# A bidirectional state-space scan in an encoder trunk: the order of the state product, one PSUM bank, the norm's second half and two empty steps

## The chip, the cores and the metric

The kernel runs on one core of a Trainium2 chip, as one program. The metric is the device time of one execution in microseconds (us); lower is better. The engines are named as in the profile: PE (TensorE, matmuls; PEld is its weight load), DVE (VectorE), ACT (ScalarE), POOL (GpSimd) and SP, whose queue issues most transfers. Each runs its own list of instructions in order and waits on semaphores. Matmuls write to PSUM, which has eight banks here, each holding one tile of 128 x 512 float32.

## The reference

Two layers (DEPTH) of an encoder trunk work on 16 meta tokens and 1024 tokens of 1024 features (L = 1040). Each layer normalises, projects once, splits the columns over four groups (pooling, a 2-D Fourier transform, a bidirectional state-space scan, attention), gates them, projects back and adds to the residual. The change touches the scan. Cut to what matters:

```python
def ssd_direction(xh, dt, a, bm, cm):          # one direction, in chunks
    xdt = xh * dt; cs = cumsum(dt * a)         # within a chunk
    cb = einsum("bclgn,bcsgn->bcgls", cc, bc)  # C.B, masked, times exp(cs_t - cs_s)
    y_diag = einsum("bcgrls,bcsgrp->bclgrp", cb * lmat, xdt)
    chunk_states = einsum("bclgn,bcgrl,bclgrp->bcgrpn", bc, exp(cs_end - cs), xdt)
    h_next = h * exp(cs_end) + chunk_states    # carried from chunk to chunk
    y_off = einsum("bclgn,bcgrpn,bcgrl->bclgrp", cc, h_before_chunk, exp(cs))
    return y_diag + y_off

def ssd_mixer(...):
    y = forward + flipped backward + d_skip * x
    y = y * silu(z)
    return rmsnorm(y, norm_w)                  # over 512 features
```

Both directions have eight heads of 64 in two groups with 128 states; the step sizes `dt` are a softplus of a projection.

## The kernel before

Features lie on the partitions, tokens along the rows, and float32 products are made of three matmuls on rounded halves (`mm3`, L133 to L135). Tokens go in three chunks of 348, 346 and 346 for the projections and in NQ = 10 chunks of QC = 104 for the scan.

**Who sets the order.** The functions are generators that yield after each step. `weave` takes steps of several streams in turn by weights; `stage(gen, steps, n)` weaves a stream with n pieces of `fill2`, the output projection of the other groups (each piece 12 matmuls L133 to L135, then an add L337 or, for the attention group, a copy L334 and an add L335, between transfers). On top of that the framework orders each engine's instructions itself when the program is built, by its own estimate of times and of when buffers come free. So a line that stands later in the code can come earlier on an engine, and the order has to be read from the built program.

**PSUM.** `ps(tag)` hands out banks. The tag `mm` has two banks of its own; `sc`, `pv` and `xx` have one each. Three spare banks, y0, y1 and y2, are lent to tags by SPARE, one entry per stage. The last entry is that of the scan: y0 and y2 go to `xx`, y1 to `sc`. Tiles are named after the bank, so a tile of `xx` shows as psxx or psy in the profile, where numbers are left out.

**The step sizes** (`ssd_dt`, part D of the stream `fill` that runs beside attention): five passes of two chunks each. A pass loads its projection (L715), goes through a chain of some 20 small DVE and ACT instructions up to L744, transposes on PE (L748, L749), copies (L751) and stores.

**The backward scan** (`ssd_bwd`, nine steps): `ssd_tok` transposes a chunk of x into `sc` (L771) and of B into `xx` (L774), and copies the latter to one of three small buffers (L776). `ssd_state` scales x (L786), makes the state product on PE (L789) and adds it to the decayed state (POOL L795, DVE L796). Its buffers come from a pool that the projections of the other groups hold in part.

**The forward scan** (`ssd_fwd`) goes through two kinds of steps in turn. `prepare(q)`: transposes, the C-B product in `xx` (L854), its two masked copies (L858, L859), eight minima and exponentials (DVE L861, ACT L862), eight pairs of scaled copies and multiply-adds (ACT L865, DVE L866), and one product on POOL (L867). `finish(q)`: the backward and forward state's part of the output (`ssd_off`, PE L803, in `sc` and `pv`), evacuated by DVE L878 and L881; the state product, also in `pv`; POOL's add L886; the product with x on PE in `xx` (L892), added by L893; the skip term L895.

**The norm** (`ssd_fin`) runs once per token chunk, in two halves. The first gates and sums squares (L928 to L932). The second sums over partitions on PE (L935), takes the root by Ln and Exp on ACT (`rstd`, L139 to L146) and scales (L939). `silu_` (L300) needs a table of ACT other than Ln and Exp do, and asks for theirs again behind it (L301).

In both layers the last part of the scan is woven with the output projection of its own first two token chunks (`tail`).

Of the kernel before, what the change touches and what calls it, by code (L numbers as in the profile page):

```python
# [28 lines left out]
NQ = L // QC  # L29
# [23 lines left out]
def hybrid_trunk(ctx: ExitStack, tc: tile.TileContext, io, out, depth=DEPTH):  # L53
# [20 lines left out]
    NBIG, NBB = 30, 5  # L74
    WB = (4, 5)
    PB, KB, NPF, NACC = 2, 3, 14, 4
    SPARE = (('xx', 'xx', 'mm'), ('sc', 'sc', 'mm'), ('xx', 'mm', 'xx'), ('xx', 'sc', 'xx'))
    GK = 2
    FB = (6, 6, 0, 1, 4, 1, 6, 9)
    GA = (22, 23, 22, 13)  # L80
# [619 lines left out]
    def ssd_dt(l, s):  # L700

        s.csd = drp.tile([NQ, 2, 8, QC], F32, name=nm("csd"))
        s.ecd = drp.tile([NQ, 2, 8, QC], F32, name=nm("ecd"))
        s.ded = drp.tile([2, 8, NQ], F32, name=nm("ded"))
        s.tkd = drp.tile([NQ, QC, 144], F32, name=nm("tkd"))
        R = slice(0, 40)
        a = wp.tile([40, 1], F32, name=nm("a"), tag="a", bufs=1)
        nc.scalar.activation(a, vec(l, V_AL)[R], AF.Exp)
        nc.vector.tensor_scalar(a, a, -1.0, None, op0=ALU.mult)
        for q0 in range(0, NQ, 2):  # L710
            n = 2
            w = n * QC
            v = big()
            x, e, u, dt, t1 = [v[:, i * w:i * w + w] for i in range(5)]
            nc.sync.dma_start(x[R], s.gd["dt"][0, :, q0 * QC:q0 * QC + w])  # L715
            nc.vector.tensor_scalar(x[R], x[R], vec(l, V_DTB)[R], None, op0=ALU.add)
            nc.scalar.activation(e[R], x[R], AF.Abs)
            nc.scalar.activation(e[R], e[R], AF.Exp, scale=-1.0)
            nc.vector.tensor_scalar(u[R], e[R], 1.0, None, op0=ALU.add)
            nc.vector.scalar_tensor_tensor(e[R], u[R], 1.0, e[R], op0=ALU.subtract, op1=ALU.subtract)  # L720
            nc.scalar.activation(u[R], u[R], AF.Ln)
            nc.vector.tensor_tensor(u[R], u[R], e[R], op=ALU.subtract)
            nc.vector.scalar_tensor_tensor(dt[R], x[R], 0.0, u[R], op0=ALU.max, op1=ALU.add)
            nc.vector.tensor_scalar(x[R], dt[R], a, None, op0=ALU.mult)
            nc.vector.memset(t1[32:64], 0.0)
            for i in range(n):
                c = slice(i * QC, (i + 1) * QC)
                nc.vector.tensor_tensor_scan(t1[0:32, c], ones[0:32, :QC], x[0:32, c], 0.0, op0=ALU.mult, op1=ALU.add)
                nc.vector.tensor_tensor_scan(t1[32:40, c][:, ::-1], ones[32:40, :QC], x[32:40, c][:, ::-1], 0.0, op0=ALU.mult, op1=ALU.add)
            by_q = lambda ap: ap.rearrange("p (q t) -> p q t", t=QC)  # L730
            cs = by_q(t1[R])
            ce = wp.tile([40, 4], F32, name=nm("ce"), tag="ce", bufs=2)[:, :n]
            nc.vector.tensor_copy(ce[0:32], cs[0:32, :, QC - 1])
            nc.vector.tensor_copy(ce[32:40], cs[32:40, :, 0])
            nc.vector.tensor_tensor(by_q(e[R]), ce.unsqueeze(2).broadcast_to([40, n, QC]), cs, op=ALU.subtract)
            nc.scalar.activation(e[R], e[R], AF.Exp)
            nc.vector.tensor_tensor(t1[64:104], e[R], dt[R], op=ALU.mult)
            nc.scalar.activation(u[R], t1[R], AF.Exp)
            nc.scalar.activation(ce, ce, AF.Exp)
            for i, r in ((0, slice(0, 8)), (1, slice(32, 40))):  # L740
                nc.sync.dma_start(s.csd[q0:q0 + n, i].rearrange("q r t -> r q t"), by_q(t1[r]))
                nc.sync.dma_start(s.ecd[q0:q0 + n, i].rearrange("q r t -> r q t"), by_q(u[r]))
                nc.sync.dma_start(s.ded[i, :, q0:q0 + n], ce[r])
            nc.vector.tensor_scalar(t1[R], t1[R], -1.0, None, op0=ALU.mult)  # L744
            p = ps("xx")
            for i in range(n):
                c = slice(i * QC, (i + 1) * QC)
                nc.tensor.transpose(p[:QC, 144 * i:144 * i + 104], t1[:104, c], ident[:104, :104])  # L748
                nc.tensor.transpose(p[:QC, 144 * i + 104:144 * i + 144], dt[:40, c], ident[:40, :40])  # L749
            t = sm("s")  # L750
            nc.scalar.copy(t[:QC, :144 * n], p[:QC, :144 * n])  # L751
            nc.sync.dma_start(s.tkd[q0:q0 + n].rearrange("q t c -> t q c"), t[:QC, :144 * n].rearrange("t (q c) -> t q c", c=144))
            yield
# [81 lines left out]
    def ssd_fwd(l, s):  # L835
# [34 lines left out]
        def finish(q, st):  # L870
            qs = slice(q * QC, (q + 1) * QC)
            xt, xw, bt, rb = ready.pop(q)
            e = vr(big())
            for a in range(2):
                nc.sync.dma_start(e[64 * a:64 * a + 64].rearrange("p (i j) t -> p i j t", i=2), s.ecd[q, :, 4 * a:4 * a + 4].partition_broadcast(64))
            if q < NQ - 1:
                pb = ssd_off(s, q, s.sb[q], "sc")
                nc.vector.tensor_tensor(e[:, 4:8], pb.rearrange("p (j t) -> p j t", t=QC), e[:, 4:8], op=ALU.mult)  # L878
            if q > 0:
                pf = ssd_off(s, q, st, "pv")  # L880
                nc.vector.tensor_tensor(e[:, 0:4], pf.rearrange("p (j t) -> p j t", t=QC), e[:, 0:4], op=ALU.mult)  # L881
            new = None
            if q < NQ - 1:
                new = ssd_state(s, 0, q, xt, bt, st, xw, s.sf[:, 512 * (q % 2):512 * (q % 2) + 512])
            if 0 < q < NQ - 1:
                nc.gpsimd.tensor_tensor(e[:, 0:4], e[:, 0:4], e[:, 4:8], op=ALU.add)  # L886
            y = e[:, 4:8] if q == 0 else e[:, 0:4]
            pd = ps("xx")
            for h in range(8):
                j, a = h // 2, h % 2  # L890
                r = 4 * a + j
                nc.tensor.matmul(pd[64 * a:64 * a + 64, j * QC:(j + 1) * QC], xt[:, h * 64:h * 64 + 64], rb[:, r], start=True, stop=True)  # L892
            nc.vector.tensor_tensor(y, y, pd[:, :4 * QC].rearrange("p (j t) -> p j t", t=QC), op=ALU.add)  # L893
            for j in range(4):
                nc.vector.scalar_tensor_tensor(s.y[j][:, qs], s.xbc[j][:, qs], vec(l, V_DS + j), y[:, j], op0=ALU.mult, op1=ALU.add)  # L895
            return new

        s.sf = big()
        st = norm = None
        for q in range(NQ + 1):  # L900
            if q < NQ:
                prepare(q)
            if norm is not None:
                next(norm, None)
                norm = None
            if q < NQ:
                yield
            if q:
                st = finish(q - 1, st)
                ci = next((i for i, (c0, cw) in enumerate(CH) if (q - 1) * QC < c0 + cw <= q * QC), None)  # L910
                if ci is not None:
                    norm = ssd_fin(l, s, ci)
# [67 lines left out]
    for l in range(depth):  # L980
        s = S()
# [173 lines left out]
```

## Time and profile before

| | |
|---|---|
| median of 3 runs | 2183.52 us (2173.6 to 2186.84) |
| the profiled execution | 2183.98 us, span 2181.9 us |
| mean granted TensorE clock | 0.964 |
| backward scan, layers 0 and 1 | about 860 to 930 and 1935 to 2008 us of the span |
| forward scan | about 930 to 1085 and 2008 to 2160 us |
| step sizes | about 424 to 462 and 1505 to 1543 us |
| matmuls, PE | 11868 records, 2002.1 us busy |

The profile is of one execution. A row of a list of groups reads: line, engine, operation, output and inputs, shape, count, then busy time, mean ns of one, and the idle time of the engine ahead of it with what ended it. A row of a list of waits reads: who waited for whom, us in total, times, longest. Lines are those of the kernel before. In the changed kernel those behind L744 are higher by 2 (so L748, L776, L789, L796, L861, L866, L867, L892 and L893 are L750, L778, L791, L798, L863, L868, L869, L894 and L895 there), the evacuations L878 and L881 are L883 and L886, and the norm's lines are higher by 1.

### The profile page before, as it was taken

To read this page: it belongs to the slowest core of one execution; us is meant where nothing else is said; L and a number is where in the kernel's file an instruction comes from. 1 tells how busy PE (TensorE), PEld (TensorE's weight loads), DVE (VectorE), ACT (ScalarE), POOL (GpSimd) and SP (SyncE) were. 2 spreads that over 40 slices of the span, in tenths; PEclk is the share of its full clock that TensorE was granted. 3 is DMA by queue.
4 is the path that set the end of the run, shared out by engine and by line. 5 is a ranking of instruction groups with operands and counts; after the bars stand their busy time and mean duration, and the time that the engine had idled before them with its cause. 6 is when DMAs were issued, how large, how long until landed. Compare 5 with 4: busy or idle time off the path is not lost. (4 is left out here: it accounts for less than half of the span.)

```text
span 2181.9 us, 33618 instructions
## 1 busy us (share of the span) xinstructions
PE 2002.1 (92%) x11868; PEld 1755.1 (80%) x11868; DVE 1323.7 (61%) x2614; ACT 1004.6 (46%) x2191; POOL 642.0 (29%) x642
## 2 busy tenths in 40 slices
PE   6699999989999999988976999999999999988888
PEld 5498888867899868877864988888778997878778
DVE  6373535558566355689864735256576554466996
ACT  5335254444443456346443353444435425463562
POOL 3005235135131220245220142441442304112550
PEclk9799999999999999999997999999999999999999
DMA  4321222113224478776743212121223335776666
GB/s 131 103 86 61 59 66 74 36 56 95 94 81 137 126 217 267 195 186 187 223 125 108 88 59 68 64 63 34 76 81 99 124 113 149 246 231 179 176 190 188
DMA packets 170374, 269.48 MB, mean 124 GB/s; under 512 B 21522, under 2 KB 117334, under 8 KB 170206
## 3 DMA queue, kind: packets, MB, share of 16 engines
q1 hardware_dynamic: 167550, 258.01, 39.0%
q0 software_dynamic: 2656, 9.33, 1.7%
q8 instruction: 93, 1.52, 0.3%
q14 instruction: 75, 0.61, 0.1%
HBM read 189.27 MB, written 73.77 MB: 121 GB/s over the span
## 5 line engine op out<-in xcount | busy, mean ns | idle before, releaser
L133 PE MATMUL psmm<-big,wh 128*128 128x346 f32 (+2 forms) x1920 | 639.8, 333 | 27.0 <-ACT sms L334 9.2
L134 PE MATMUL psmm<-big,wh 128*128 128x346 f32 (+2 forms) x1920 | 629.7, 328 | 7.7 <-DVE big L130 4.0
L135 PE MATMUL psmm<-big,wl 128*128 128x346 f32 (+2 forms) x1920 | 626.3, 326 | 2.0 <-DVE wl L130 2.0
L646 POOL TENSOR_TENSOR acc<-acc,pf 116x346 f32<-116x346 f32 (+4 forms) x336 | 343.9, 1048 | 531.6 <-ACT pf L637 531.5
L133 PEld LDWEIGHTS psmm<-big,wh 128*128 128x128 f32 x1920 | 367.9, 192 | 62.2 <-issue 21.7
L134 PEld LDWEIGHTS psmm<-big,wh 128*128 128x128 f32 x1920 | 368.2, 192 | 19.5 <-DVE big L130 8.4
L135 PEld LDWEIGHTS psmm<-big,wl 128*128 128x128 f32 x1920 | 368.3, 192 | 6.3 <-DVE wl L130 2.6
L130 DVE TENSOR_TENSOR wl<-wr,wh 128x512 fp32r<-128x512 f32 x232 | 182.8, 792 | 215.2 <-ACT wh L129 214.2
L129 ACT CAST wh<-wr 128x512 fp32r<-128x512 f32 (+1 forms) x236 | 145.0, 616 | 270.9 <-PE psmm L134 216.7
L133 PE MATMUL psy<-big,wh 128*128 128x346 f32 (+2 forms) x672 | 224.1, 334 | 0.0
L134 PE MATMUL psy<-big,wh 128*128 128x346 f32 (+2 forms) x672 | 223.1, 332 | 1.1 <-POOL big L182 0.7
L135 PE MATMUL psy<-big,wl 128*128 128x346 f32 (+2 forms) x672 | 219.2, 326 | 0.0
L606 DVE TENSOR_REDUCE mx<-psy 128x1 f32<-128x346 f32 (+3 forms) x272 | 132.8, 512 | 56.1 <-PE psy L605 55.4
L637 ACT ACTIVATE pf<-psy 116x346 f32<-116x346 f32 (+4 forms) x288 | 125.6, 457 | 80.3 <-PE psy L635 77.2
L656 PE MATMUL pspv<-pf,vt 116*64 116x346 f32 (+5 forms) x864 | 160.6, 463 | 0.0
L133 PEld LDWEIGHTS psy<-big,wh 128*128 128x128 f32 x672 | 129.9, 193 | 10.9 <-issue 8.8
L134 PEld LDWEIGHTS psy<-big,wh 128*128 128x128 f32 x672 | 130.0, 193 | 8.5 <-DVE big L130 2.8
L135 PEld LDWEIGHTS psy<-big,wl 128*128 128x128 f32 x672 | 130.3, 194 | 1.3 <-issue 0.8
L606 DVE TENSOR_REDUCE mx<-pssc 128x1 f32<-128x346 f32 (+3 forms) x136 | 69.9, 514 | 69.3 <-PE pssc L605 68.4
L337 DVE TENSOR_TENSOR sms<-sms,psmm 128x346 f32<-128x346 f32 (+2 forms) x128 | 65.1, 511 | 73.7 <-PE psmm L135 43.8
L656 PEld LDWEIGHTS pspv<-pf,vt 116*64 116x64 f32 (+1 forms) x864 | 58.6, 136 | 61.5 <-issue 24.0
L634 PE MATMUL psy<-big,big 128*116 128x346 f32 (+4 forms) x288 | 95.8, 334 | 8.1 <-DVE mx L606 7.2
(285 smaller groups left out, 3331.3 us busy)
## 6 DMA issues: line engine op xcount, KB each, us to landing
wr<-w SPq DMA_DIRECT2D x248, 256.0 KB
hd<-sms SPq DMA_DIRECT2D x112, 173.0 KB
sms<-hd SPq DMA_DIRECT2D x112, 173.0 KB
bb<-csd SPq DMA_DIRECT2D x40, 338.0 KB
md<-big SPq DMA_DIRECT2D x24, 520.0 KB
gd<-sms SPq DMA_DIRECT2D x64, 173.0 KB
big<-gd SPq DMA_DIRECT2D x16, 520.0 KB
big<-md SPq DMA_DIRECT2D x16, 520.0 KB
```

What stands on the lines that cost most here:

```text
L129: nc.scalar.copy(hi, src)
L130: nc.vector.tensor_tensor(lo, src, f(hi), op=ALU.subtract)
L133: nc.tensor.matmul(out_ps, ah, bh, start=start, stop=False)
L134: nc.tensor.matmul(out_ps, ah, bl, start=False, stop=False)
L135: nc.tensor.matmul(out_ps, al, bh, start=False, stop=stop)
L337: nc.vector.tensor_tensor(ht, ht, p[:, :cw], op=ALU.add)
L606: nc.vector.tensor_reduce(mx[:qn, q, e, ci:ci + 1], p[:qn, :cw], axis=AX.X, op=ALU.max)
L634: nc.tensor.matmul(p[:n, :cw], k1[:, k0:k0 + n], s1[e][:, cs], start=True, stop=False)
L637: nc.scalar.activation(pf[:n, :cw], p[:n, :cw], AF.Exp, scale=0.125)
L646: nc.gpsimd.tensor_tensor(accs[c0, e][:n, :cw], accs[c0, e][:n, :cw], pf[:n, :cw], op=ALU.add)
L656: nc.tensor.matmul(hold["pv"][64 * e:64 * e + 64, :cw], s.vt[:n, k, v, :], pfs[e][:n, :cw], start=(k == 0), stop=(k == len(KTS) - 1))
```

## The change

Four edits. The last entry of SPARE lends y2 to `pv` instead of `xx`: in the scan `pv` has two banks and `xx` two (one and three before). In `finish` the state product and its update are issued ahead of the backward and forward parts of the output instead of behind them. The norm's second half is issued after the next `finish` instead of ahead of it, and behind the yield. `ssd_dt` yields twice, with nothing issued between, ahead of the transposes.

```diff
-    SPARE = (('xx', 'xx', 'mm'), ('sc', 'sc', 'mm'), ('xx', 'mm', 'xx'), ('xx', 'sc', 'xx'))
+    SPARE = (('xx', 'xx', 'mm'), ('sc', 'sc', 'mm'), ('xx', 'mm', 'xx'), ('xx', 'sc', 'pv'))
@@ ssd_dt
             nc.vector.tensor_scalar(t1[R], t1[R], -1.0, None, op0=ALU.mult)
+            yield
+            yield
             p = ps("xx")
@@ finish
+            new = None
+            if q < NQ - 1:
+                new = ssd_state(s, 0, q, xt, bt, st, xw, s.sf[:, 512 * (q % 2):512 * (q % 2) + 512])
             if q < NQ - 1:
                 pb = ssd_off(s, q, s.sb[q], "sc")
                 nc.vector.tensor_tensor(e[:, 4:8], pb.rearrange("p (j t) -> p j t", t=QC), e[:, 4:8], op=ALU.mult)
             if q > 0:
                 pf = ssd_off(s, q, st, "pv")
                 nc.vector.tensor_tensor(e[:, 0:4], pf.rearrange("p (j t) -> p j t", t=QC), e[:, 0:4], op=ALU.mult)
-            new = None
-            if q < NQ - 1:
-                new = ssd_state(s, 0, q, xt, bt, st, xw, s.sf[:, 512 * (q % 2):512 * (q % 2) + 512])
@@ the loop over q
             if q < NQ:
                 prepare(q)
-            if norm is not None:
-                next(norm, None)
-                norm = None
-            if q < NQ:
                 yield
             if q:
                 st = finish(q - 1, st)
+                if norm is not None:
+                    next(norm, None)
+                    norm = None
```

What the built program makes of it, at three places.

On PE, in layer 0, near the end of the backward scan. L774 (now L776) are transposes of B, L771 (L773) of x, L789 (L791) state products; psmm marks fill. L854 (L856) on psxx_8916 is the C-B product of forward step 0. Before:

```order
L774 MATMUL psy_8909<-ct,big_8176 104x128
L774 MATMUL psy_8909<-ct,big_8177 104x128
L789 MATMUL pspv_8694<-big_8691,smq_8689 128x256 x2
L771 MATMUL pssc_8777<-ct,big_8172 104x128
L771 MATMUL pssc_8777<-ct,big_8173 104x128
L771 MATMUL pssc_8777<-ct,big_8174 104x128
L771 MATMUL pssc_8777<-ct,big_8175 104x128
L854 MATMUL psxx_8916<-big_8178,big_8176 104x104
L854 MATMUL psxx_8916<-big_8179,big_8177 104x104
L133 MATMUL psmm_8666<-big_8224,wh_8606 128x346
L134 MATMUL psmm_8666<-big_8225,wh_8606 128x346
```

Now:

```order
L134 MATMUL psmm_9227<-big_8240,wh_9132 128x346
L135 MATMUL psmm_9227<-big_8239,wl_9133 128x346
L133 MATMUL psmm_9288<-big_8548,wh_9282 128x348
L856 MATMUL psxx_8916<-big_8178,big_8176 104x104
L856 MATMUL psxx_8916<-big_8179,big_8177 104x104
L805 MATMUL pssc_9093<-big_8178,big_8847 128x104
L791 MATMUL psy_9089<-big_8914,smq_8912 128x256 x2
```

Step 0's C-B product has moved from ahead of a long run of fill (the one that writes psmm_8666 to psmm_9227) to behind it, next to the first `finish`. The products of steps 1 and 2, which stood within that run, have moved behind it as well, and layer 1 has the same.

On DVE, in layer 0, what follows those products. L858 and L859 (now L860, L861) are the masked copies, L866 (L868) the multiply-adds, bb_8901 belongs to step 0 and bb_8990 to step 1; L337 evacuates fill, L130 splits its weights. Before, at the start of the run of fill:

```order
L858 TENSOR_TENSOR cfb_8919<-psxx_8916,ct 104x208
L859 TENSOR_TENSOR cfb_8919<-psxx_8916,ct 104x208
L337 TENSOR_TENSOR sms_8664<-sms_8664,psmm_8666 128x346
L130 TENSOR_TENSOR wl_9133<-wr_9130,wh_9132 128x512
L866 SCALAR_TENSOR_TENSOR bb_8901<-cfb_8919,big_8166,bb_8901 104x104 x4
L337 TENSOR_TENSOR sms_8706<-sms_8706,psmm_8708 128x348
L866 SCALAR_TENSOR_TENSOR bb_8901<-cfb_8919,big_8166,bb_8901 104x104 x4
```

Now, behind it (L798 adds a state product, L883 evacuates a backward part, L788 scales x):

```order
L337 TENSOR_TENSOR sms_9225<-sms_9225,psmm_9227 128x346
L860 TENSOR_TENSOR cfb_8919<-psxx_8916,ct 104x208
L861 TENSOR_TENSOR cfb_8919<-psxx_8916,ct 104x208
L788 TENSOR_TENSOR big_9003<-big_9003,big_8166 104x4x64 x2
L130 TENSOR_TENSOR wl_9848<-wr_9845,wh_9847 128x512
L868 SCALAR_TENSOR_TENSOR bb_8901<-cfb_8919,big_8166,bb_8901 104x104 x8
L883 TENSOR_TENSOR big_9084<-pssc_9093,big_9084 128x416
L860 TENSOR_TENSOR cfb_9008<-psxx_9005,ct 104x208
L861 TENSOR_TENSOR cfb_9008<-psxx_9005,ct 104x208
L798 TENSOR_TENSOR big_8899<-big_8899,pspv_9247 128x512
L868 SCALAR_TENSOR_TENSOR bb_8990<-cfb_9008,big_8166,bb_8990 104x104 x5
```

The work of steps 0 and 1 has moved from among the evacuations of fill to among the first `finish` steps.

On ACT, in layer 0, at the second norm. z is gated by L300; L139 and L141 are Ln and Exp of the norm; L334 copies fill. Before:

```order
L300 ACT_TABLE_LOAD
L300 ACTIVATE z_10182<-z_10182 128x4x346
L334 COPY sms_9841<-psmm_9828 128x346
L301 ACT_TABLE_LOAD
L776 COPY smq_9882<-psy_9879 104x256
```

Now:

```order
L300 ACT_TABLE_LOAD
L300 ACTIVATE z_10182<-z_10182 128x4x346
L334 COPY sms_9750<-psmm_9737 128x348
L334 COPY sms_9769<-psmm_9756 128x346
L139 ACT_TABLE_LOAD
L139 ACTIVATE smn_9813<-psxx_9811,epst 128x348
L778 COPY smq_9882<-psy_9879 104x256
L141 ACT_TABLE_LOAD
L141 ACTIVATE smn_9815<-smn_9813 128x348
```

The first norm's Ln and Exp now follow the second norm's gate directly, ahead of the preload L301, and each loads a table of its own. The whole program has 68 table loads, 55 before. At the step-size transposes 59 and 60 matmuls (layers 0 and 1) stood between the last score product of the first attention pair and the first transpose; now 62 and 61 do.

## The prediction

> **What bounds the kernel now.** I read the page's shares first, then the stretches, then who waits for whom. The page says that TensorE is the busiest engine:
>
> ```profile
> PE 2002.1 (92%) x11868; PEld 1755.1 (80%) x11868; DVE 1323.7 (61%) x2614; ACT 1004.6 (46%) x2191; POOL 642.0 (29%) x642
> ```
>
> An average hides stages, so here are the stretches around the scan. The columns are length, then busy time (and instructions) of PE, PEld, DVE, ACT and POOL, the granted clock, the DMA share and GB/s.
>
> ```profile
> 896.00:928.00 32.00, 29.20 (x186) 28.53 (x184) 18.09 (x48) 11.56 (x35) 6.39 (x6) 1.00 0.75 201
> 928.00:1030.00 102.00, 85.63 (x591) 77.44 (x591) 95.11 (x216) 54.47 (x152) 52.47 (x49) 0.95 0.66 185
> 1030.00:1060.00 30.00, 29.01 (x196) 26.98 (x195) 28.28 (x63) 18.46 (x44) 11.46 (x9) 0.95 0.65 179
> 1060.00:1085.00 25.00, 21.12 (x132) 20.08 (x131) 16.27 (x38) 8.99 (x19) 2.19 (x3) 0.93 0.91 273
> 1975.00:2006.00 31.00, 28.36 (x173) 27.64 (x171) 15.47 (x41) 8.47 (x25) 5.58 (x5) 0.94 0.74 202
> 2006.00:2115.00 109.00, 92.63 (x658) 84.00 (x658) 100.04 (x233) 62.31 (x177) 57.17 (x51) 0.95 0.70 183
> 2115.00:2160.00 45.00, 39.61 (x253) 36.82 (x252) 37.23 (x79) 18.00 (x36) 8.35 (x8) 0.92 0.69 194
> ```
>
> In the forward scans (928 to 1030 and 2006 to 2115) VectorE (DVE) is busy 93% and 92%, TensorE (PE) only 84% and 85%: **the scan is bound by DVE**. Just ahead of each scan (896 to 928, 1975 to 2006) it is the other way round: PE runs fill at 91%, and DVE has 14 and 16 us free. The change aims at PE's waits:
>
> ```profile
> PE pspv L789 <- DVE big L881: 18.2, 9, 4.3
> PE psy L935 <- DVE sms L932: 9.2, 4, 2.9
> PE psxx L748 <- DVE big L744: 6.9, 4, 3.7
> ```
>
> The first is the state product waiting for its one bank, the second the norm's sum, the third the step-size transposes: 34.3 us in all, 1.6% of the span. But the first two waits are waits for an engine that is itself full. Removing them lets PE come earlier to the next thing that DVE has not done. What the scan can gain is DVE's own idle time:
>
> ```profile
> DVE big L893 <- POOL big L886: 2.4, 2, 1.2
> DVE sms L337 <- DMA sms<-hd: 2.1, 1, 2.1
> DVE big L878 <- DMA big<-ecd: 2.0, 2, 1.7
> DVE big L786 <- ACT big L851: 1.9, 2, 1.7
> DVE big L796 <- PE pspv L789: 0.6, 2, 0.4
> ...
> DVE big L893 <- POOL big L886: 3.4, 3, 1.2
> DVE big L878 <- DMA big<-ecd: 3.0, 2, 2.0
> DVE big L786 <- ACT big L851: 1.6, 1, 1.6
> ```
>
> These are DVE's waits in the two scans, the first five from layer 0. Only 0.6 us of them is a wait for the state product (L796), which the new order brings forward; the rest is for POOL, DMA and ACT.
>
> **The change part by part.** *The bank moved from the ring of xx to that of pv.* Every wait for L881 goes, since the state product and the forward product now have a bank each. The price is in the ring of xx, which falls from three banks to two. In the backward scan a step's B transposes (L774, now L776) hold a bank of xx until ACT copies them to one of three small buffers, and the backward steps stand still while the fill runs. Before, a third bank let the C-B products of forward steps 0, 1 and 2 (L854) go out ahead of and between the fill. By the instruction order shown with the change they now stand behind it (L856). So their DVE work leaves the stretch with free time and lands in the full one: per layer 6 mask products (L858, L859), the 19 of 24 multiplies L866 that stood ahead of the last backward steps, and 8 of L861 (step 2's minima). Their durations in the two scans, layer 0 first:
>
> ```profile
> L861 DVE SCALAR_TENSOR_TENSOR bb<-bb,gap,bb 104x104 f32<-104x104 f32 x53 | 26.7, 551 | 0.0
> L866 DVE SCALAR_TENSOR_TENSOR bb<-cfb,big,bb 104x104 f32<-104x104 f32 x45 | 14.4, 380 | 0.0
> L858 DVE TENSOR_TENSOR cfb<-psxx,ct 104x208 f32<-104x208 f32 x3 | 1.1, 364 | 0.0
> ...
> L861 DVE SCALAR_TENSOR_TENSOR bb<-bb,gap,bb 104x104 f32<-104x104 f32 x56 | 26.4, 515 | 0.4 <-DMA bb<-csd 0.3
> L866 DVE SCALAR_TENSOR_TENSOR bb<-cfb,big,bb 104x104 f32<-104x104 f32 x53 | 15.7, 355 | 0.0
> ```
>
> Layer 0: 19 x 0.380 + 6 x 0.364 + 8 x 0.551 = 7.2 + 2.2 + 4.4 = 13.8 us. Layer 1, with L858 as before: 19 x 0.355 + 2.2 + 8 x 0.515 = 6.7 + 2.2 + 4.1 = 13.0 us. Together **+26.8 us** of DVE work where DVE is the bound. The cover that hid it was the fill on PE, and that cover is gone.
>
> Against this, an engine that is behind waits less. If DVE arrives later, its waits for DMA and for POOL's add shrink: 2.4 + 2.1 + 2.0 = 6.5 us in layer 0 and 3.4 + 3.0 = 6.4 us in layer 1, **-12.9 us** if all of them go. They need not (0 is the other end); I take all, because the new order also puts three L863 between the forward product's evacuation and the sum that waits for POOL.
>
> *State product first.* The same 2 matmuls, decay multiplies and add, so no work is added. The add (L796, now L798) moves ahead of the two evacuations (L878, L881). I cost this at nothing: DVE has the step's multiplies to do meanwhile. Were that cover gone, the evacuations would wait for one state product and one backward product in each of 18 steps; at the 0.6 us which DVE waits for PE in layer 0 that would be at most 11 us.
>
> *The norm's second half after the finish.* No DVE work changes. But ScalarE's order now puts Ln and Exp between the SiLU and the preload that follows it, and the program has 68 table loads instead of 55. Their price:
>
> ```profile
> L300 ACT ACT_TABLE_LOAD x24 | 30.8, 1283 | 0.4
> L301 ACT ACT_TABLE_LOAD x22 | 28.2, 1283 | 0.4
> ```
>
> 13 x 1.283 = 16.7 us of ACT, of which seven loads (9.0 us) stand in the scans. ACT is busy 53% and 57% there (54.47 of 102, 62.31 of 109), so I take 0, with 9 us as the other end.
>
> *The empty steps.* The wait here is after a load:
>
> ```profile
> 423.95 1.82 SPq L715 DMA_DIRECT2D big<-gd  x5
> ...
> 435.75 0.32 PE L134 MATMUL psmm<-big,wh 128*128 128x346 f32 x1
> 435.91 0.32 PE L135 MATMUL psmm<-big,wl 128*128 128x346 f32 x1
> 438.67 0.30 PE L748 MATMUL psxx<-ct,big 104*104 104x104 f32 x1 [2.45 <-DVE big L744]
> ...
> 1520.34 0.30 PE L748 MATMUL psxx<-ct,big 104*104 104x104 f32 x1 [3.75 <-DVE big L744]
> ```
>
> The loads L715 are issued when head pair 0's last score product has freed the five buffers, so what hides DVE's chain is the matmuls between that product and the first transpose. I counted them in the built order: 59 before and 62 now in layer 0, 60 and 61 in layer 1. At 0.16 us each (435.75 to 435.91) that is 4 x 0.16 = **-0.6 us**. The later transposes stand a little closer than before (99 and 100 matmuls between the first and the last become 94 and 94). I take -0.6; the ends are -6.9 (all of that wait) and +2 (11 fewer matmuls to cover, 1.8 us). Ten fill pieces move from the earlier head pairs into the last one; PE does them in either place, so I put that at 0.
>
> **The sum.** 26.8 - 12.9 - 0.6 = +13.3 us. The profiled execution took 2183.98 us (span 2181.9 and 2.1 around it), 0.5 above the median of 2183.52. So 2183.98 + 13.3 = 2197.3; I say **2197**.
>
> **The rivals.**
>
> *Faster: the waits simply go.* If DVE's fullness is only an effect of PE arriving late, the whole 34.3 us are to be had (2150) or about half (2167). For it: L881's waits are long, up to 4.3 us, and recur. Against: DVE's busy time alone is 95.1 of 102 us. The Trainium skill, "Perfetto Trace Analysis", Optimization Strategy, says that the same gap repeating on the engine that should be saturated can mean too few buffers, SBUF or PSUM; by it a second bank is the cure. The trace agrees that the gap repeats (9 times), but PE is not the engine that is saturated there. Chance 0.19; in 0.09 by more than 1%.
>
> *Slower: DVE is held up further by POOL.* The first steps' POOL products (L867) move into the scan as well, where POOL and DVE disturb each other:
>
> ```profile
> L867 POOL TENSOR_TENSOR bb<-bb,bb 104x832 f32<-104x832 f32 x10 | 20.5, 2048 | 30.8 <-DVE bb L866 30.8
> ...
> 941.40 1.99 DVE L861 SCALAR_TENSOR_TENSOR bb<-bb,gap,bb 104x104 f32<-104x104 f32 x8
> ...
> 953.67 4.13 DVE L861 SCALAR_TENSOR_TENSOR bb<-bb,gap,bb 104x104 f32<-104x104 f32 x3
> ```
>
> Eight L861 took 1.99 us while POOL was idle, and three took 4.13 us beside L867. Two such products per layer, those of steps 0 and 1, move in: 4 x 2.05 = 8.2 us if DVE loses all of it. DVE's idle time would then stay too, since POOL's add comes later: 2197 + 8 + 13 = 2218. It decides where L867 comes to run beside L863, as in the last row, rather than beside DVE's other work. The Trainium skill, "SBUF — State Buffer", SBUF: two separate sides, describes an exclusive lock on the port pair that DVE and GpSimd share: the second to come "fully blocks". The 4.13 us agree with blocking. Against this rival: the means that I used contain such blocking already, from six products in 102 us. Chance 0.26, counted as over 1%.
>
> *The change does nothing:* the scheduler's order absorbs it, since the fill is movable; 2184. Against it: the C-B rows have visibly moved. Chance 0.12.
>
> **How the numbers follow.** My forecast (2197, with the ends of its terms about 2185 to 2205) has 0.43. Its case, nothing (0.12) and the lesser gain (0.10) are within 1%, 21.8 us, which is about what a measurement of this kernel can tell from no change: 0.65. Faster by more 0.09, slower by more 0.26. The range must leave out no more than 0.2: below 2174 lie the large gains and a little of the lesser ones (0.12), and above 2217 the slower rival's end at which little of the idle time is recovered (0.08).
>
> **What would show it.** Right: no PE wait at the state product for L886 (the new number of L881); no L868 in the fill ahead of the scan and DVE idle there for longer than 14 us; PE's new waits at the y product (L894) of steps 0 to 2 for POOL's L869, some us each; DVE busy 95% or more from the last backward step on, and the scan longer by 5 to 10 us; the wait at L750 about as before. Wrong: a scan shorter than 102 and 109 us, or DVE below 90% in it.

## The result, and the profile after

| | median, us | ratio to before, 95% interval |
|---|---|---|
| before, beside it on the same chip | 2185.18 | |
| changed | 2209.00 (2203.59 to 2213.35) | 1.0112 (1.0087 to 1.0137) |

The changed kernel is slower by 1.1%, 24.5 us by the ratio (19 to 30). The forecast was 2197, +13.3 us: the direction was right, and the size was half. The profiled execution took 2211.45 us, with a span of 2209.7 (2181.9 before).

The page's first line says almost nothing. PE has 6 us more, ACT 22 us more (16.7 of them are 13 further table loads of 1.283 us), DVE 7 us less:

```profile
PE 2008.5 (91%) x11868; PEld 1760.4 (80%) x11868; DVE 1317.0 (60%) x2614; ACT 1027.0 (46%) x2204; POOL 645.9 (29%) x642
```

So one has to cut the span into stages. These are the forward scans, from the first product of L803 (after: L805) to the last y product. Before:

```profile
934.65:1068.15 133.50, 117.43 (x828) 107.96 (x826) 120.58 (x273) 73.00 (x195) 60.77 (x56) 0.96 0.67 186
2011.92:2146.17 134.25, 116.97 (x828) 107.32 (x826) 121.23 (x275) 72.78 (x195) 63.44 (x56) 0.95 0.70 186
```

The same two scans after, each behind a row of some 32 us of the fill ahead of it; in layer 0 that row ends 6.7 us before the scan begins (columns: length, then PE, PEld, DVE, ACT and POOL with instructions, granted clock, DMA share, GB/s):

```profile
899.00:931.50 32.50, 32.50 (x193) 32.04 (x193) 11.27 (x21) 3.85 (x7) 2.41 (x4) 0.93 0.65 184
938.18:1082.57 144.39, 119.88 (x838) 108.72 (x836) 132.76 (x310) 87.63 (x230) 67.69 (x58) 0.96 0.65 178
1998.00:2029.47 31.47, 30.43 (x197) 29.52 (x195) 13.06 (x26) 5.19 (x10) 3.16 (x6) 1.00 0.75 203
2029.47:2172.52 143.05, 122.10 (x838) 111.82 (x836) 130.88 (x310) 85.74 (x229) 69.57 (x58) 0.93 0.64 177
```

The scans are longer by 10.9 and 8.8 us, with 37 and 35 DVE instructions more; in the fill ahead of them DVE is busy for only 11 and 13 us. That is the displacement that the forecast described. It shows at the head of the scans: before, the first y product came 0.6 and 1.1 us ahead of the first L803, and after, 7.1 us behind the first L805 in both layers, since step 0's displaced DVE work stands between. From the first to the last y product the scans take 134.1 and 135.4 us before, and 137.2 and 135.9 after, so 16 of the 19.7 us lie there. Among DVE's groups in layer 0's scan, before and then after:

```profile
L861 DVE SCALAR_TENSOR_TENSOR bb<-bb,gap,bb 104x104 f32<-104x104 f32 x56 | 27.5, 538 | 0.0
L866 DVE SCALAR_TENSOR_TENSOR bb<-cfb,big,bb 104x104 f32<-104x104 f32 x56 | 16.5, 354 | 0.0
```

```profile
L863 DVE SCALAR_TENSOR_TENSOR bb<-bb,gap,bb 104x104 f32<-104x104 f32 x64 | 38.5, 651 | 0.0
L868 DVE SCALAR_TENSOR_TENSOR bb<-cfb,big,bb 104x104 f32<-104x104 f32 x80 | 26.9, 393 | 1.0 <-ACT bb L867 1.0
```

PE no longer waits for L886 at the state product. In layer 0's scan it waits for the y sum L895 instead, ahead of the next step's C-B product and B transposes, which share the two banks of xx with the y product:

```profile
PE psy L856 <- DVE big L895: 7.0, 2, 3.5
PE psy L776 <- DVE big L895: 3.8, 2, 2.3
PE psxx L856 <- DVE big L895: 3.0, 3, 2.1
...
PE psxx L894 <- POOL bb L869: 2.2, 1, 2.2
PE psy L894 <- POOL bb L869: 1.9, 2, 1.1
```

The other part of the loss is where the forecast had put nothing. Attention goes through four pairs of heads, a stretch for each, with fill beside them. The second, third and fourth stretch of layer 0, before and then after:

```profile
291.20:424.60 133.40, 132.16 (x793) 114.12 (x793) 60.54 (x112) 58.64 (x126) 51.05 (x54) 1.00 0.18 59
424.60:588.10 163.50, 153.39 (x849) 126.45 (x849) 116.28 (x233) 76.85 (x174) 59.51 (x55) 0.96 0.24 75
588.10:779.80 191.70, 188.70 (x1134) 167.24 (x1136) 102.67 (x165) 86.92 (x179) 50.71 (x47) 1.00 0.39 124
```

```profile
287.50:414.50 127.00, 125.76 (x748) 105.93 (x748) 60.49 (x110) 57.80 (x124) 51.62 (x54) 1.00 0.20 61
414.50:575.60 161.10, 152.33 (x856) 125.33 (x857) 111.71 (x227) 76.30 (x171) 59.25 (x55) 0.97 0.23 71
575.60:778.90 203.30, 196.26 (x1167) 175.66 (x1166) 100.30 (x168) 92.17 (x184) 54.41 (x48) 0.99 0.36 115
```

The second and third pair give back 6.4 and 2.4 us, the fourth takes 11.6. PE's idle time in the fourth rises from 3.0 to 7.0 us, most of it at one place, products of the pooling group that wait for ACT's split of their input (before, then after):

```profile
PE psxx L133 <- ACT smn L129: 1.2, 1, 1.2
```

```profile
PE psxx L133 <- ACT smn L129: 6.2, 3, 2.6
```

The stage that follows, from attention's last product to the backward scan's first state product, is longer too: 82.9 and 79.2 us before,

```profile
782.80:865.70 82.90, 74.67 (x432) 66.73 (x432) 46.33 (x90) 51.26 (x80) 4.78 (x9) 0.96 0.81 253
1858.50:1937.70 79.20, 72.72 (x434) 65.03 (x434) 45.15 (x88) 50.84 (x80) 4.89 (x8) 0.98 0.82 258
```

and 84.9 and 84.3 after:

```profile
782.60:867.50 84.90, 74.29 (x433) 67.41 (x430) 45.43 (x88) 51.92 (x81) 2.73 (x5) 0.94 0.83 258
1873.60:1957.90 84.30, 72.53 (x431) 65.61 (x428) 46.72 (x91) 52.30 (x81) 3.22 (x7) 0.96 0.85 260
```

In layer 1 the same three head pairs take 479.70 us before and 480.70 after:

```profile
1375.80:1855.50 479.70, 464.28 (x2754) 402.83 (x2754) 267.44 (x491) 218.48 (x469) 158.39 (x157) 0.99 0.29 91
```

```profile
1389.20:1869.90 480.70, 464.98 (x2748) 402.18 (x2746) 264.05 (x487) 221.78 (x469) 160.01 (x158) 0.99 0.27 88
```

So this part is 2.8 + 2.0 us in layer 0 and 1.0 + 5.1 in layer 1, 10.9 in all, beside 19.7 in the scans. The rest of the span gave some us back. All these rows are of one execution of each kernel, and a stretch which an edit leaves alone moves too: from attention's last product to the first L803 it is 151.8 and 153.4 us before, and 155.0 and 156.4 in norm_only (below), whose edit acts later. What a stretch is worth is therefore taken from several kernels where that can be done.

### The profile page after: what moved, and what is told of

The parts are those of the page before. It is cut to its first block, busy times and chain, and to the rows that moved or that the text cites. A ratio compares the mean times of both kernels' runs of the same rounds, so it can differ in the third digit from the quotient of the medians.

```text
span 2209.7 us, 33668 instructions
## 1 busy us (share of the span) xinstructions
PE 2008.5 (91%) x11868; PEld 1760.4 (80%) x11868; DVE 1317.0 (60%) x2614; ACT 1027.0 (46%) x2204; POOL 645.9 (29%) x642
## 5 line engine op out<-in xcount | busy, mean ns | idle before, releaser
L133 PE MATMUL psmm<-big,wh 128*128 128x346 f32 (+2 forms) x1920 | 641.8, 334 | 16.5 <-ACT sms L334 8.2
L130 DVE TENSOR_TENSOR wl<-wr,wh 128x512 fp32r<-128x512 f32 x232 | 180.4, 782 | 252.5 <-ACT wh L129 251.9
L129 ACT CAST wh<-wr 128x512 fp32r<-128x512 f32 (+1 forms) x236 | 144.7, 616 | 265.5 <-PE psmm L134 192.6
L133 PEld LDWEIGHTS psy<-big,wh 128*128 128x128 f32 x672 | 129.3, 192 | 19.9 <-issue 12.2
L337 DVE TENSOR_TENSOR sms<-sms,psmm 128x346 f32<-128x346 f32 (+2 forms) x128 | 64.9, 510 | 90.5 <-PE psmm L135 49.6
L797 POOL TENSOR_TENSOR big<-big,decb 128x256 f32<-128x256 f32 x64 | 41.5, 668 | 224.1 <-DVE big L798 104.3
```

The source lines that it names most:

```text
L129: nc.scalar.copy(hi, src)
L130: nc.vector.tensor_tensor(lo, src, f(hi), op=ALU.subtract)
L133: nc.tensor.matmul(out_ps, ah, bh, start=start, stop=False)
L337: nc.vector.tensor_tensor(ht, ht, p[:, :cw], op=ALU.add)
L797: nc.gpsimd.tensor_tensor(hv(new)[:, :, a], hv(st)[:, :, a], d[:, :, a].unsqueeze(2).broadcast_to([128, 4, 64]), op=ALU.mult)
```

## The experiments

A gain or loss in us is the ratio of the comparison times 2183, with its 95% interval. "The scans" are the stretch from the first L803 to the last y product; only the rows of bank_from_step3 begin at its first y product, 1.1 and 0.6 us ahead of that.

### Each edit alone

bank_only, the kernel before with

```diff
-('xx', 'sc', 'xx'))
+('xx', 'sc', 'pv'))
```

> Only the bank moves from the ring of xx to that of pv; the order of the step, the norm and the step-size transposes stay as before. Theory A (the bank carries the whole loss, since the C-B products of steps 0 to 2 stand behind the fill and their VectorE work lands in the full scan): 20 to 28 us slower than before, about 2205, with the forward scans longer by 8 to 11 us each. Theory B (the forecast's 13 us for the bank is right, and the other 11 come from the other three edits): 11 to 15 us slower, about 2197. Theory C (the bank is a gain, and the loss comes from the other edits): 2184 or less.

Measured: 2204.51, +22 us (18 to 26). The rows of its two scans:

```profile
931.95:1080.12 148.17, 123.32 (x838) 111.47 (x836) 138.71 (x313) 83.12 (x227) 67.64 (x58) 0.93 0.61 173
2018.03:2167.70 149.67, 124.98 (x838) 113.72 (x836) 137.85 (x311) 80.27 (x225) 68.74 (x58) 0.90 0.60 167
```

The time is theory A's, but the scans are longer by 14.7 and 15.4 us and not by 8 to 11, more than in the whole change. So the edits aren't additive, and one of the others takes something back.

state_only, with the `new = ...` block of `finish` ahead of the two `ssd_off`:

> Only the state product is issued ahead of the two other products of the step; xx keeps three banks and pv one. Theory A: within 4 us of before (2180 to 2188), since the C-B products stay in the fill and VectorE has as much to do as before; the forward product must now wait for the state's add in the one bank of pv. Theory B: 4 to 11 us slower, because the evacuations on VectorE wait behind the state's add.

Measured: 2185.94, +5 us (2 to 9). A small loss, which the interval doesn't give to A or B alone; the wait moved to L803, which now waits for the add L796 in the one bank of pv (9.2 us in layer 0's scan).

norm_only, with `next(norm, None)` behind `finish`:

> Only the norm's second half is issued after the next finish. Theory A: within 3 us of before; ACT has table loads more but stands idle 40% of the scan. Theory B: 4 to 9 us slower, the price of seven ACT table loads of 1.28 us in the scans, with the last scan steps waiting for ACT.

Measured: 2181.85, +0.4 us (-2 to +3). Theory A. But the run doesn't price the change's table loads: its trace has 57, two more than before, while empty_only has 61, no_empty 62 and the whole change 68. Most of the 13 come with the other edits.

empty_only, with

```diff
             nc.vector.tensor_scalar(t1[R], t1[R], -1.0, None, op0=ALU.mult)
+            yield
+            yield
             p = ps("xx")
```

> Only the two empty steps ahead of the step-size transposes. Theory A: within 3 us of before; the wait of the transposes shrinks by about 2.6 us at most. Theory B: 4 to 8 us slower, with the FFT stage of layer 1 longer by about 5 us, because fill pieces moved out of the first head pairs are missing later.

Measured: 2193.48, **+13 us** (10 to 15). Slower as in theory B, and by more than it said: two lines that issue nothing cost 0.6%. But the FFT stage of layer 1, where B put the loss (from attention's last product to the first state product), is longer by 2 us and not 5. Its fourth head pairs take 203.6 and 203.1 us, against 191.7 and 191.0 before.

### What the empty steps do

`FN` says how many steps of fill are run beside each head pair, and an empty step counts as one. Two yields in five passes are ten steps, so ten pieces fewer (57 PE products) are done beside the second pair, and they are left for the fourth.

```diff
-    FN = (10, 17, 17, 17, 28)
+    FN = (10, 17, 19.5, 17, 28)
...
-            n = FN[t + 1] * PC
+            n = int(FN[t + 1] * PC)
```

empty_more_fill has the empty steps and this edit:

> The two empty steps alone, and ten fill steps more beside the second head pair, so that the pieces displaced by empty steps are done there and the last head pair begins with as much fill left as before (2856 TensorE products into the program in both). Theory F (the empty steps cost because ten fill pieces move into the last head pair, whose norm and pool groups and whose following FFT stage then wait for ACT): no slower than 3 us over before, 2180 to 2186, with a last head pair of 191 to 193 us (203.6 with the empty steps alone). Theory G (the empty steps themselves, the place of the transposes or of the loads): still 8 to 13 us slower.

Measured: 2182.75, -1 us (-4 to +2). fill_late is the kernel before, with 14.5 in the place of 19.5 and no empty step:

> The kernel before without any empty step, with ten fill steps fewer beside the second head pair, so that the same pieces move into the last head pair as by the empty steps (it begins 2799 products into the program in both). Theory F: 9 to 13 us slower than before, as the empty steps alone. Theory G: within 3 us of before.

Measured: 2194.19, +12 us (9 to 15). Theory F holds from both sides: the loss is there without any empty step, and gone with them in place. It is the place of the ten pieces, and neither the empty steps themselves nor the place of the transposes or loads (theory G). fill_late's head pairs are those of the changed kernel:

```profile
289.30:416.10 126.80, 124.65 (x748) 105.65 (x746) 60.06 (x110) 57.44 (x124) 52.73 (x54) 1.00 0.20 61
416.10:576.70 160.60, 150.94 (x857) 123.84 (x857) 112.09 (x227) 76.12 (x172) 59.67 (x55) 0.98 0.24 71
576.70:779.90 203.20, 196.23 (x1167) 175.65 (x1166) 99.58 (x168) 92.39 (x184) 53.60 (x48) 0.99 0.36 116
```

Where the 12 us go can be read from all the traces together. Four kernels have the ten pieces late (fill_late, empty_only, bank_from_step3 below and the changed kernel). Their three head pairs take 490.6 to 491.4 us in layer 0 and 480.3 to 482.5 in layer 1, and those of the twelve kernels with the pieces in the old place 487.8 to 490.8 and 477.8 to 480.2: some 4 us for both layers. The stage behind attention takes 84.9 to 85.9 us in layer 0 in the four, and 78.5 to 83.6 in the other sixteen; in layer 1 it is 81.6 to 84.3 and 79.1 to 82.9, which overlap: by the means some 6 us for both layers. In layer 0 PE waits there for ACT's copies and splits of the transform (L507, L129), 7.2 to 8.9 us in the four and 2.7 to 6.3 in the others. Before, and then fill_late:

```profile
PE psy L133 <- ACT big L507: 2.0, 1, 2.0
PE psy L133 <- ACT big L129: 1.9, 1, 1.9
```

```profile
PE psy L133 <- ACT big L129: 5.0, 1, 5.0
PE psy L133 <- ACT big L507: 3.0, 1, 3.0
```

Why ACT is later there no run tests.

no_empty is the changed kernel without its two yields:

> The changed kernel without the two empty steps: bank, state first and norm are in. If the empty steps cost as much here as alone (12.9 us): 2194 to 2199. If they cost nothing beside the other three: 2205 to 2211. The attention's fourth head pair should be shorter by about 12 us, its second and third together longer by 9, as in the kernel before.

Measured: 2196.98, +14 us (11 to 18): the first case. Its fourth head pair of layer 0 is 10.2 us shorter than the changed kernel's, the second and third together 9.6 longer. after_more_fill is the changed kernel with the edit of `FN` above:

> The changed kernel with all four edits, and ten fill steps more beside the second head pair. Theory F: the empty steps' share of 11 us goes, 2195 to 2199, as the changed kernel without them. Theory G: 2204 to 2210.

Measured: 2193.54, +9 us (6 to 12): theory F again, 1.5 us below its range. Of the change's 24.5 us, then, 10 (no_empty) to 15 (this run) belong to the place of ten fill pieces.

fill_early is the kernel before with 19.5 and no empty step, the same shift the other way:

> The kernel before with ten fill steps more beside the second head pair, so that the last head pair begins 54 TensorE products later in the program (2910 instead of 2856). If the fill's place costs in proportion (theory F, linear): 8 to 12 us faster than before, about 2172. If the last head pair is well covered already and only overfilling it costs: within 4 us of before.

Measured: 2171.91, **-13.5 us** (-18 to -9), faster than both kernels, as the linear theory F says and by 1.5 us more. Its head pairs in layer 0:

```profile
289.10:424.80 135.70, 131.66 (x756) 106.01 (x755) 71.41 (x150) 56.29 (x133) 52.49 (x54) 1.00 0.18 57
424.80:588.50 163.70, 158.48 (x935) 138.52 (x934) 108.19 (x198) 81.13 (x168) 55.46 (x54) 0.99 0.23 77
588.50:769.90 181.40, 179.92 (x1081) 158.51 (x1079) 96.54 (x162) 86.70 (x178) 49.19 (x46) 1.00 0.41 135
```

The third pair is as long as before (163.7 against 163.5) with 86 products more in it, and the fourth is 10 us shorter. PE's idle time in the third pair falls from 10.1 to 5.2 us: there, fill was nearly free. In the fourth it costs its full length. The three head pairs are 7.8 us shorter in layer 0 and 5.3 in layer 1, which is nearly the whole gain.

### What the bank does

xx_lost takes y2 from xx and gives it to nobody, bank_lost gives it to the fill's ring (mm):

```diff
-('xx', 'sc', 'xx'))
+('xx', 'sc', 'none'))      # xx_lost;  'mm' in bank_lost
```

> The kernel before with the third bank of xx taken away and given to nobody. Theory A (the displaced C-B work costs about 20 us of VectorE time a layer, and in the run in which the fill's products had the bank their faster fill paid for most of it): 12 to 22 us slower than before. Theory E (the loss of xx costs little, and the second bank of pv itself does the harm): within 6 us of before.

> The kernel before, whose xx loses its third bank, while pv does not gain it (it goes to the ring of the fill's products). Theory A and D: what hurts is xx's loss, so 18 to 30 us slower than before (2200 to 2212). Theory E (it is the second bank of pv that hurts, by letting the state's add come earlier and in a worse place on VectorE): within 6 us of before.

Measured: xx_lost 2194.82, +12 us (8 to 15), the low end of A's range; bank_lost 2186.55, +3 us (0 to 6). bank_lost alone would have spoken for theory E; xx_lost shows that it was wrong to read it so. A third bank for the fill's products is worth 8.5 us, the difference of the two, and it had hidden most of xx's loss. Here are xx_lost's scans:

```profile
927.13:1072.72 145.59, 125.00 (x838) 114.43 (x836) 140.25 (x313) 83.12 (x227) 68.56 (x58) 0.92 0.66 178
2010.05:2154.51 144.46, 123.57 (x838) 113.09 (x836) 137.80 (x313) 82.75 (x227) 69.29 (x58) 0.92 0.65 176
```

DVE has 19.7 and 16.6 us more work in them than before, and its idle time falls from 12.9 and 13.0 us to 5.3 and 6.7. This is the forecast's account in its pure form: work moved in, idle time recovered (13.9 us; the forecast took 12.9).

bank_from_step3 is the changed kernel, but xx keeps three banks until forward step 3 is prepared:

```diff
-('xx', 'sc', 'pv'))
+('xx', 'sc', 'xx'))
...
         def prepare(q):
+            if q == 3:
+                phase["spare"] = ('xx', 'sc', 'pv')
```

> The changed kernel with all four edits, but xx keeps its third bank until forward step 3 is prepared, and pv gets it from there. Theory A (the loss is the C-B work of steps 0 to 2 that is pushed out of the fill): its products stand in the fill again, so most of the bank's 22 us come back and the empty steps' 10 to 13 us stay: 2188 to 2196, with forward scans of 133 to 136 us from the first off product to the last y product as before (after: 144 and 143). Theory D (two banks of xx are too few in the scan itself, since each step's C-B product then waits for the step before to sum its y on VectorE): the scans stay at 140 us and more, and the time at 2202 to 2212.

Measured: 2198.39, +16 us (13 to 19), between the ranges of A and D. With the C-B products back in the fill, the scans are nearly those of before:

```profile
938.50:1074.50 136.00, 118.25 (x830) 110.79 (x830) 120.39 (x275) 75.93 (x198) 63.30 (x57) 0.94 0.67 185
2022.90:2160.90 138.00, 118.57 (x831) 109.18 (x830) 119.53 (x274) 76.96 (x198) 64.07 (x56) 0.94 0.65 175
```

133.5 and 134.3 us before, 144.4 and 143.1 after, 135.0 and 137.4 here when counted from the first L805 as well: of 19.7 us lost in the scans 15.1 come back with the first steps' work. DVE is no busier in them than before, so the other 4.6 are idle time of DVE. They would be theory D's, the two-bank ring in the scan itself; no run takes them apart from what pv's second bank does there. The empty steps' loss stays.

cb_in_pv has the bank and state first, and takes the C-B product from pv:

```diff
-            pc = ps("xx")
+            pc = ps("pv")
```

> Bank and state first alone, with the C-B product taken from the ring of pv (two banks) and not from that of xx (two banks). By the instruction order the C-B products of steps 0 and 1 stand in the fill again and no C-B product shares a ring with the y product. Theory A: the bank's loss is gone, 2178 to 2190. Theory D: gone too, since no C-B product waits for y any more; but if it is the scan's own ring that matters, the scans become shorter than before, below 133 us, and the time 2170 to 2180. If two banks of xx hurt in another way (the B transposes held up behind y): 2195 and more.

Measured: 2191.03, +8 us (5 to 11), 1 us above A's range and far from D's. It is 6 us better than no_empty, so part of the bank's loss seems to go when steps 0 and 1 stand in the fill (the intervals, 5 to 11 and 11 to 18, just touch); the scans stay at 141 and 138 us.

### The state product and pv's second bank

xx_lost_state is xx_lost with the state product first:

> State product first, xx with two banks, pv with one. If the state product first costs 5 us in a ring of one bank, as it did alone: 2198 to 2202, and the second bank of pv is then worth 2 to 5 us in the new order (2197 with it), against a loss of 11 us in the old one. If the new order helps whatever pv has: 2186 to 2192.

Measured: 2192.17, +8.5 us (5.5 to 11.6): the second case, at its upper end. With xx at two banks:

| | pv one bank | pv two banks |
|---|---|---|
| old order | +12 (xx_lost) | +22 (bank_only) |
| state product first | +8.5 (xx_lost_state) | +14 (no_empty, with the norm's edit) |

The second bank of pv, the point of the edit, costs 11 us in the old order (the intervals don't meet) and about 6 in the new one (they overlap by 1 us). It gains in neither. The waits show what it buys. Over the whole run, xx_lost and then bank_only:

```profile
PE pspv L789 <- DVE big L881: 19.7, 11, 2.8
...
PE psxx L854 <- DVE big L893: 2.0, 2, 1.8
```

```profile
PE psxx L854 <- DVE big L893: 10.4, 6, 3.7
PE psy L854 <- DVE big L893: 10.1, 3, 4.6
```

19.7 us of waiting for DVE at the state product became 20.5 us of waiting for DVE at the C-B product. PE meets the same full engine at another product. Why the second place is dearer isn't shown by a run of its own: DVE's idle time in the scans is 9.5 and 11.8 us with the bank and 5.3 and 6.7 without.

### Two attempts to take the work away

before_no_early and xx_lost_no_early leave out the multiplies of the first three steps:

```diff
-                nc.vector.scalar_tensor_tensor(rb[:, r], cf[:, g], ...
+                if q > 2:
+                    nc.vector.scalar_tensor_tensor(rb[:, r], cf[:, g], ...
```

> The kernel before without the 24 VectorE multiplies of forward steps 0 to 2 in each layer (L866): left out of the computation, to read what they cost. Theory A (they are hidden in the fill): 0 to 6 us faster than before, since 19 of the 24 stand in the fill, where VectorE is free. Against A: 10 us and more faster.

> The kernel whose xx has lost its third bank, without the same 24 multiplies a layer (left out of the computation). Theory A (they now stand where VectorE is the bound): at least 14 us faster than that kernel with them (2194.8), thus 2170 to 2181, since 24 of them take 24 x 0.41 = 9.8 us a layer; the difference to before without them shrinks to 0 to 5 us. Theory D (waits of the two-bank ring): still 8 to 12 us above before without them.

Measured: before_no_early 2192.19, +8 us (5 to 11); xx_lost_no_early 2190.07, +5 us (2 to 8), 7 below xx_lost by the ratios (4.8 by the medians). Both miss theory A, the first in its direction and the second in its size. Less work made the kernel before slower, and the other one faster by about a third of the work taken away (48 x 0.42 = 20 us). The difference between the two kernels fell from +12 to -2 us, by more than A said; but a removal with a side effect of +8 us is no clean measure. The side effect isn't explained; what can be seen is that DVE waits longer for transfers in the stretch around the first scan, here 185 us of before_no_early,

```profile
DVE sms L337 <- DMA sms<-hd: 20.3, 12, 4.6
DVE bb L861 <- DMA bb<-csd: 7.5, 5, 1.8
```

and 175 us of before:

```profile
DVE sms L337 <- DMA sms<-hd: 7.2, 5, 2.1
...
DVE bb L861 <- DMA bb<-csd: 2.3, 1, 2.3
```

### A better version

mm_for_sc gives the fill's products the third bank at the cost of sc:

```diff
-('xx', 'sc', 'xx'))
+('xx', 'mm', 'xx'))
```

> The kernel before, whose fill products get a third bank in the backward and forward scan, taken from the ring of sc (which keeps one) and not from that of xx. If the fill's third bank is worth 8 us also here and sc's second bank little: 2172 to 2178, faster than before. If the token transposes and the backward product, which share the one bank of sc, now wait for each other: 2186 to 2200.

Measured: 2176.08, -8 us (-11 to -5): the first case. Its scans are no shorter than before (135.5 and 134.7 us), so where the gain lies is open. both is fill_early with that edit:

> The kernel before with ten fill steps more beside the second head pair and the fill's third bank taken from the ring of sc. If the two gains, 13.5 and 7.9 us, add up, since one lies in the attention and one in the scans: 2160 to 2165. If they are one gain (PE's idle time in the fill): 2170 to 2173.

Measured: 2167.88, -17.5 us (-24 to -11). The fastest median of all. But 2167.88 lies between the two ranges, and the interval covers both the sum, -21.4, and fill_early's -13.5 alone, so whether the two gains add up stays open.

## Why the prediction was half right

**The bound and the mechanism: right.** The bound was DVE, the waits for L881 were not there to be had, and the C-B work of the first steps came into the scan.

**The bank's sum: right by luck.** The forecast without the empty steps was 26.8 - 12.9 = +13.9; the change without them measured +14 (11 to 18). But the bank alone measured 22 (18 to 26), and the state product first, which I had put at 0, took 8 of it back. Two terms were off, and they cancelled.

**The terms inside it: off, in opposite directions too.** In the scans as counted here all 24 multiplies of a layer came in (80 against 56); the forecast's 19 are the same work counted from 928 us, where five of the 24 stood in the scan already. They and the minima took more time than the forecast said: in layer 0 (38.5 - 27.5) + (26.9 - 16.5) = 21.4 us where it had 7.2 + 4.4. Other DVE groups got cheaper, so the scans' DVE time rose by 12.2 and 9.7 us, 21.8 in all, against 26.8. The idle time was hardly recovered: 12.9 and 13.0 us before, 11.6 and 12.2 after, 2.1 us where I took 12.9. So the scans are 19.7 us longer, not 13.9. That the idle time can be recovered is shown by xx_lost (13.9 us); with pv's second bank it isn't.

Against these 19.7 us something came back ahead of the scans. In layer 1 the stretch from attention's last product to the first L803 takes 146.8 to 151.0 us in the six kernels with the work displaced and the ten pieces not late (no_empty, after_more_fill, xx_lost, bank_only, xx_lost_state, xx_lost_no_early), and 152.5 to 156.4 in six that keep the work in the fill (before, norm_only, state_only, empty_more_fill, before_no_early, fill_early). So the place that the work left wasn't quite free. In layer 0 the two groups overlap. Layer 1's backward scan, before and in xx_lost:

```profile
1937.69:2011.92 74.23, 64.19 (x372) 59.52 (x372) 44.22 (x106) 23.25 (x62) 15.04 (x19) 0.93 0.65 180
```

```profile
1942.50:2010.05 67.55, 60.91 (x364) 56.87 (x363) 33.87 (x68) 15.10 (x32) 10.35 (x16) 0.95 0.70 188
```

The stretch is 6.7 us shorter here, with 10 us less of DVE (no_empty: 68.2, the changed kernel 71.5). In layer 0 it was 68.9 us before and 69.7 in xx_lost, so nothing. That DVE's work is the reason isn't shown by a run of its own.

**The rival with POOL: partly true.** Its row of 4.13 us doesn't price one L867: the three L861 stood beside L867, L886 and L335, which POOL ran one after the other from 953.50 to 957.43 us. But POOL does hold DVE up. Over all twenty traces 6304 multiplies and minima of this kind were taken (104x104, the lines L861 and L866 of each kernel); the 4666 with no POOL instruction beside them took at most 0.331 us, and each of the 873 that took over 0.34 us had one beside it. If every DVE instruction of the two scans is set against the shortest of its line and shape, those beside POOL took longer by 29.1 and 27.4 us before, and 32.7 and 31.3 after: 7.5 us more, near the 8.2 that the rival gave. They are part of the 21.8 above and don't come on top. And most of DVE's idle time stayed, as the rival said.

**State product first at 0: mis-sized where it stood.** +5 us alone, -3 beside a two-bank xx (intervals that overlap), but -8 with pv's second bank, which is the case of the change.

**The norm at 0: right**, +0.4. The 13 table loads that I charged to it were not its own: alone it adds two.

**The empty steps at -0.6: the step that failed.** Not the wait of the transposes, which went from 6.9 to 4.3 us, but the sentence on the ten fill pieces: "PE does them in either place, so I put that at 0". It measured 10 to 15 us in the change, 13 alone, and 12 without any empty step. PE does them in either place, but the third pair had 10 us of PE's time to spare and the fourth 3, and pieces that leave the second pair (133.40 us, 132.16 busy) pull hardly any into the third's gaps (856 products against 849). In the head pairs lie nearly all of fill_early's gain and some 4 us of the loss. The rows for that were in the trace of before; I cut it into stretches around the scan alone. Some 6 us more lie in the stage behind attention, where PE then waits longer for ACT; why it does stays open. With 10 to 13 us for this step the sum would have been 24 to 27, and the measured loss is 24.5; that it fits so closely rests on the luck with the bank.

**What it named as signs.** Seen: no PE wait for L886 at the state product; DVE idle ahead of the scan for 21 us of 32.5 and 18 of 31.5; waits of L894 for L869 (4.1 us in layer 0's scan); no L868 in the fill ahead of the scan (the first starts at 940.5 us). Not seen: DVE at 95% (it was 92% and 91%), and L750's wait about as before (it fell from 6.9 to 4.3 us). The scans grew by 8.8 and 10.9 us, at the upper end of 5 to 10 and just beyond it.

## What to carry to other kernels

Before a PSUM bank is moved, ask whom the waiting engine will meet next: here 20 us of waiting for DVE at one product became 20 us at another, and the bank's former owner lost the work that it had hidden in the fill. When steps drive a budget of filler, an empty step is an edit of the budget: compare PE's idle time in the stretches that lose and gain filler. A borrowed resource has two prices, that of the loser and that of the gainer, and they need a run each (bank_lost hid 8.5 us until xx_lost gave the bank to nobody).

## What I had not expected

Leaving out 48 DVE multiplies made the kernel before slower by 8 us. The same instruction on the same shape had another mean in another kernel, without a change of its own: L786 took 583 and 572 ns in xx_lost's scans and 743 in bank_only's second:

```profile
L786 DVE TENSOR_TENSOR big<-big,big 104x256 f32<-104x256 f32 x17 | 9.3, 583 | 0.0
```

```profile
L786 DVE TENSOR_TENSOR big<-big,big 104x256 f32<-104x256 f32 x17 | 12.2, 743 | 0.0
```

The traces tell the two kinds apart: with no POOL instruction beside it, L786 took 0.41 to 0.42 us in both kernels, and each of the nine that took 0.90 us and more stood beside one. So a mean from the stage before is an estimate that can be a quarter off in the stage after; the time without POOL beside it, and what is lost beside POOL, are better taken apart. That POOL's instruction is the cause is read from the times alone; no run takes it away.
